# A head's scores as two 128-row products of stacked operands, and the sums of the logs moved amid the gated linear units

## The chip, the cores and the metric

The kernel runs on one core of a Trainium2 chip. It is one program for a transformer of two two-layer blocks (512 tokens, width 1024, float32). The metric is the device time of one execution in microseconds, the median of several runs. Lower is better.

## The reference

The change touches only the mixer of the last layer, `odd_mixer`. It joins two things: an attention with forget gates (8 heads of 64) and a gated convolution over 31 positions.

```
def odd_mixer(x, w_in, forget_b, dw_w, dw_b, cn_g, cn_b, w_out):
    p = x @ w_in                                   # q, k, v: 512 each; 8 forget logits; 2 x 512
    log_f = log_sigmoid(p[..., 1536:1544] + forget_b)
    y_c = forgetting_attention(q, k, v, log_f)
    y_d = conformer_conv(p[..., 1544:], dw_w, dw_b, cn_g, cn_b)
    return concatenate([y_c, y_d]) @ w_out

def forgetting_attention(q, k, v, log_f):
    cum = cumsum(log_f, axis=1)                    # per head
    for each block of 128 queries (q0, q1):
        logits = q[q0:q1] . k[:q1] / sqrt(64)
        logits = logits + cum[q0:q1, None] - cum[None, :q1]
        logits = where(key <= query, logits, -1e30)
        out = softmax(logits) . v[:q1]

def conformer_conv(p_d, dw_w, dw_b, cn_g, cn_b):
    h = p_d[..., :512] * sigmoid(p_d[..., 512:])   # the gated linear unit
    h = causal_dwconv(h, dw_w) + dw_b              # 31 taps per channel
    return silu(layer_norm(h, cn_g, cn_b))
```

## The kernel before, in words

Every float32 product is made from three fp32r products. Each operand is cut into a high part (rounded to fp32r by ScalarE) and a low part (the rest, a subtraction on VectorE, or on GpSimd for the weights named in `ONPOOL`), and `mm3` (L369 to L373) adds high·high, high·low and low·high in PSUM. Weights come by DMA in units of up to 1024 columns and are split one or two units ahead (L170 on ScalarE, L171 on VectorE or GpSimd). The plan of the weights fixes the order in which they are loaded, and `OTHERWISE` names by number the units split on the other engine.

In `odd()` the channels lie on the partitions in four groups of 128, the tokens along the free axis. The order of the instructions is written out by hand, as a sequence of `step(taps, us)`. A step first takes some `us` microseconds of TensorE products out of a list of waiting projections (`fill`), then emits the work that earlier steps left with `done` (evictions, the softmax of a block), then splits a weight unit if fewer than `AHEAD` are ready, then emits `taps` taps of the convolution on VectorE (`tap`, L1376, one fused multiply-add of 128x512 each; channel groups 0 to 2 in turn) and a share of a tap of group 3, which ScalarE multiplies into a tile `tp` (L1381) and GpSimd adds to the sum `cv` (L1382).

The order in the mixer before:

- The gates of channel groups 0 and 1 (their products ran at the end of the layer before), then the products of the gated linear units 2 and 3 (`glu`, 96 products of 512 columns) in steps of 1.8 taps.
- The values and the forget logits (`od_v`, 4 units, 96 products of 264 columns), then on VectorE and ScalarE the log of the sigmoid as a chain of small operations on 128x32 (`log_sigmoid`).
- 32 products of the first pair of heads' queries and keys (`pair(0)`), then `sums()`: two small products that sum the logs over the tokens. They wait for the log chain. VectorE then adds the blocks up and `spread(0)` lays the cumulative sums (high and low part) and ones into the tiles `ab`, which TensorE transposes (`rows(0)`) into four bias rows per head for heads 0 to 3. Heads 4 to 7 follow in `rows(1)` during head 1.
- The heads, one after the other: in the turn of head h TensorE makes the scores of head h+1 block by block (128, 256, 384, 512 keys), attends head h to the values, and transposes the probabilities of head h+1; the projections of later pairs, of the other values and of the output are the filling.

A block of scores is five products into one PSUM bank (L1574 to L1576): three fp32r products over the 64 rows of the head (high and low of query and key: `qh`, `ql`, and the same for keys), one product over the 4 bias rows (L1575), and the causal mask as a bf16 product with the identity over 128 columns. Two heads share a projection: head 2p lies on partitions 0 to 63 of the `pair` tiles, head 2p+1 on 64 to 127. One split of 128x512 on ScalarE (L381 or L378) and one on VectorE (L382 or L379) serve both heads.

In the trace PE is TensorE, DVE VectorE, ACT ScalarE, POOL GpSimd.

Of the kernel before, what the change touches and what calls it, by code (L numbers as in the profile page):

```python
# [9 lines left out]
F32 = mybir.dt.float32  # L10
# [32 lines left out]
for _k, _w in (("g_q", 3), ("g_kv", 2), ("g_sub", 1), ("conv_w", 12), ("pool_s", 4), ("dw_w", 124),  # L43
# [11 lines left out]
OTHERWISE = (11, 12, 15, 20, 23, 24, 25, 73, 79, 80, 81, 82, 83, 84, 85, 86, 88, 90, 91, 100, 102, 103, 224, 226, 231)  # L55
# [9 lines left out]
    "pre": (2.6, 3.4, 2.2, 2.2),  # L65
    "glu": 1.8,
    "v": 2.5,
    "pool0": 0.35,
# [169 lines left out]
def weight_plan(a):  # L238
# [53 lines left out]
    for j in range(4):  # L292
        if j < 2:
            add("od_a", a["od_d"][0, j])
        add("od_g" if j < 2 else "od_x", a["od_d"][1, j])
        if j > 1:
            add("od_x", a["od_d"][0, j])
    for u in range(4):
        add("od_v", a["od_v0"][u])
    for x in "0" + ORDER:  # L300
# [13 lines left out]
def kernel(ctx: ExitStack, tc: tile.TileContext, a: dict, out: bass.AP):  # L314
# [1011 lines left out]
    def odd(xT, open_x, FIRST, names):  # L1326
        with pool("odd") as op_:
# [42 lines left out]
            def tap(j, k, pool=False):  # L1370
                w, x = par("dw_w", CONV * j + k), gl[j][:, k:k + S]
                if not pool:
                    if k == 0:
                        nc.vector.tensor_scalar(cv[j], x, w, par("dw_b", j), op0=OP.mult, op1=OP.add)
                    else:
                        nc.vector.scalar_tensor_tensor(cv[j], x, w, cv[j], op0=OP.mult, op1=OP.add)  # L1376
                elif k == 0:
                    nc.scalar.activation(cv[j], x, AF.Identity, scale=w, bias=par("dw_b", j))
                else:
                    tp = op_.tile([P, S], F32, name="tp", tag="tp", bufs=2)  # L1380
                    nc.scalar.activation(tp, x, AF.Copy, scale=w)  # L1381
                    nc.gpsimd.tensor_add(cv[j], cv[j], tp)  # L1382
# [49 lines left out]

            def pair(p):
                got = []
                while p > 1 and 2 * p - 3 not in SCORED:
                    yield None
                for s in range(2):
                    ps = acc()
                    yield from steps_T(ps, ("od_q", "od_k")[s])
                    hi = ov.tile([P, S], F32R, name="qh", tag=f"qh{s}", bufs=2)  # L1440
                    lo = ov.tile([P, S], F32R, name="ql", tag=f"ql{s}", bufs=2)
                    got += [hi, lo]
                    done(lambda hi=hi, lo=lo, ps=ps, s=s: split(hi, lo, ps, -0.125 if s == 0 else None))
                done(lambda: Q.update({p: got}))
                MADE.add(p)
# [23 lines left out]
            fill = Fill([glu(2), glu(3)])  # L1469
# [4 lines left out]
            while fill.parts:  # L1474
                step(OD["glu"], 1.3)
            fill.parts.extend([pair(0)] + [others() if x == 'v' else pair(int(x)) for x in ORDER])
# [23 lines left out]
            def sums():  # L1500
# [6 lines left out]
                def add():  # L1507
# [7 lines left out]
                    spread(0)  # L1515
# [7 lines left out]
            ab = [op_.tile([P, NT, 4, 32], F32, name=f"ab{i}", tag=("yh", "yl")[i], bufs=4) for i in range(2)]  # L1523
            for i in range(2):
                nc.gpsimd.memset(ab[i], 0.0)
                nc.gpsimd.memset(ab[i][:, :, :, 2 * i:2 * i + 2], 1.0)
            AB = {}

            def spread(g):
                c, h = cum[:, :, 4 * g:4 * g + 4], f32(cumh[:, :, 4 * g:4 * g + 4])  # L1530
                nc.vector.tensor_copy(ab[1][:, :, :, 0], h)
                nc.vector.tensor_sub(ab[1][:, :, :, 1], c, h)
                nc.vector.tensor_scalar(ab[0][:, :, :, 2], h, -1.0, None, op0=OP.mult)
                nc.vector.tensor_sub(ab[0][:, :, :, 3], h, c)

            def rows(g):
                for i in range(2):
                    ps = pst()
                    for t in range(NT):
                        nc.tensor.transpose(ps[:, t * P:(t + 1) * P], ab[i][:, t].rearrange("p h r -> p (h r)"), ident)  # L1540
                    AB[g, i] = op_.tile([P, S], F32R, name="rows", tag=f"rows{i}", bufs=2)
                    done(lambda x=AB[g, i], ps=ps: nc.scalar.activation(x, ps, AF.Copy))
                if g == 0:
                    done(lambda: spread(1))
# [19 lines left out]
            def score(h, qb):  # L1564
                if h > 7:
                    return
                p, i = divmod(h, 2)
                qh, ql, kh, kl = Q[p]
                ms = slice(64 * i, 64 * i + 64)
# [72 lines left out]
            rows(0)  # L1642
            step(1, 1.0)
            step(1, 1.0)
            C, OUT = [], {}
            for h in range(-1, 8):
# [5 lines left out]
                if h == 1:  # L1652
                    rows(1)
# [232 lines left out]
```

## Time and profile before

| | us |
|---|---|
| median of 3 runs (lowest, highest) | 2301.66 (2300.28, 2306.31) |
| the profiled execution | 2304.18 |
| its span | 2302.4 |
| TensorE busy over the span | 2250.3 (98%) |
| VectorE, ScalarE, GpSimd busy | 1770.4 (77%), 997.1 (43%), 471.3 (20%) |
| granted clock over the span | 0.989 |

The profile gives the busy time of each engine over a stretch, the waits with what ended them, and a timeline of single instructions. The granted clock is the share of full speed (2.4 GHz) that TensorE was given: 0.50 means 1.2 GHz. TensorE's products are pipelined, so the duration of one is longer than the distance to the next: what a product takes is read from the distance of the starts. The touched part of the mixer lies from 1701.04 us (the first product of the gated linear units) to 1891.94 us (the end of the last head's turn).

### The profile page before, as it was taken

What the parts mean: (1) busy time and instruction counts of PE and PEld (TensorE: products, weight loads), DVE (VectorE), ACT (ScalarE), POOL (GpSimd) and SP (SyncE); (2) the same over time, 40 slices, a digit from 0 to 9 for tenths busy, and PEclk for the clock granted to TensorE, in tenths of its full rate; (3) what the DMA queues carried; (4) which work ended last, traced back from release to release, by engine and by line L of the source; (5) the groups of instructions that cost most, each with busy time, mean ns of one, the idle gap of its engine ahead of it and who ended that gap; (6) DMA issues with size and microseconds to landing.
All of it is one profiled execution on the core that took longest, in us unless ns stands there. A gap on an engine that the chain in (4) does not pass through costs nothing. (4 is left out here: it accounts for less than half of the span.)

```text
span 2302.4 us, 35345 instructions
## 1 busy us (share of the span) xinstructions
PE 2250.3 (98%) x14148; PEld 1988.6 (86%) x14148; DVE 1770.4 (77%) x2718; ACT 997.1 (43%) x1665; POOL 471.3 (20%) x280
## 2 busy tenths in 40 slices
PE   8999999999999999999999999999998999999997
PEld 8878999998888789999988899999886768999996
DVE  5667888886656688888765588888767766988886
ACT  4654444333555554443333244434334654444341
POOL 2200111113321111111210011111246531111112
PEclk9999999999999999999999999999998989999999
DMA  5112233332222033333233233332232112233321
GB/s 180 55 45 92 92 106 105 111 92 90 92 66 73 28 110 101 102 110 109 86 106 100 64 129 110 110 101 92 83 96 74 37 37 101 92 110 110 101 92 65
DMA packets 59365, 210.51 MB, mean 91 GB/s; under 512 B 6624, under 2 KB 6880, under 8 KB 59200
## 3 DMA queue, kind: packets, MB, share of 16 engines
q1 hardware_dynamic: 56304, 198.97, 27.5%
q0 software_dynamic: 2320, 8.23, 1.1%
q8 instruction: 111, 1.82, 0.3%
q10 hardware_dynamic: 576, 1.05, 0.1%
q14 instruction: 54, 0.44, 0.1%
HBM read 206.12 MB, written 2.10 MB: 90 GB/s over the span
## 5 line engine op out<-in xcount | busy, mean ns | idle before, releaser
L170 ACT ACTIVATE whi<-wraw 128x1024 fp32r<-128x1024 f32 (+3 forms) x528 | 521.0, 989 | 831.0 <-PE acc L372 301.3
L171 POOL TENSOR_TENSOR wlo<-wraw,whi 128x1024 fp32r<-128x1024 f32 (+2 forms) x141 | 355.8, 2526 | 1281.4 <-ACT whi L170 1030.2
L171 DVE TENSOR_TENSOR wlo<-wraw,whi 128x1024 fp32r<-128x1024 f32 (+3 forms) x387 | 429.3, 1110 | 136.8 <-ACT whi L170 136.1
L371 PE MATMUL acc<-xh,whi 128*128 128x256 f32 (+1 forms) x1712 | 527.3, 308 | 0.0
L372 PE MATMUL acc<-xl,whi 128*128 128x256 f32 (+1 forms) x1712 | 524.2, 306 | 3.1 <-DVE xl L481 3.1
L373 PE MATMUL acc<-xh,wlo 128*128 128x256 f32 (+1 forms) x1712 | 522.8, 305 | 3.1 <-DVE wlo L171 3.1
L372 PEld LDWEIGHTS acc<-xl,whi 128*128 128x128 f32 x1712 | 322.9, 189 | 28.5 <-DVE xl L481 4.3
L371 PEld LDWEIGHTS acc<-xh,whi 128*128 128x128 f32 x1712 | 322.9, 189 | 24.8 <-issue 0.9
L373 PE MATMUL acc<-xs,wlo 128*128 128x256 f32 x1216 | 342.6, 282 | 0.0
L372 PE MATMUL acc<-xql,whi 128*128 128x256 f32 x1216 | 341.4, 281 | 0.0
L371 PE MATMUL acc<-xs,whi 128*128 128x256 f32 x1216 | 340.0, 280 | 0.4 <-ACT sums L768 0.4
L373 PEld LDWEIGHTS acc<-xh,wlo 128*128 128x128 f32 x1712 | 322.9, 189 | 20.0 <-DVE wlo L171 4.1
L371 PEld LDWEIGHTS acc<-xs,whi 128*128 128x128 f32 x1216 | 229.9, 189 | 4.4 <-ACT sums L768 0.8
L372 PEld LDWEIGHTS acc<-xql,whi 128*128 128x128 f32 x1216 | 228.5, 188 | 5.7
L373 PEld LDWEIGHTS acc<-xs,wlo 128*128 128x128 f32 x1216 | 228.4, 188 | 0.0
L371 PE MATMUL tr<-whi,hh 128*128 128x512 f32 (+1 forms) x296 | 118.1, 399 | 0.0
L372 PE MATMUL tr<-wlo,hh 128*128 128x512 f32 (+1 forms) x296 | 116.9, 395 | 0.0
L373 PE MATMUL tr<-whi,hl 128*128 128x512 f32 (+1 forms) x296 | 115.8, 391 | 0.0
L373 PE MATMUL ps<-whi,hl 128*128 128x512 f32 x288 | 113.7, 395 | 0.0
L371 PE MATMUL ps<-whi,hh 128*128 128x512 f32 x288 | 113.2, 393 | 0.0
L372 PE MATMUL ps<-wlo,hh 128*128 128x512 f32 x288 | 113.2, 393 | 0.0
L431 DVE SCALAR_TENSOR_TENSOR res<-res,acc 128x512 f32<-128x512 f32 x87 | 58.9, 683 | 55.2 <-PE acc L373 54.9
(353 smaller groups left out, 4195.6 us busy)
## 6 DMA issues: line engine op xcount, KB each, us to landing
wraw<-in_gu_dram SPq DMA_DIRECT2D x176, 512.0 KB, 3.7
wraw<-in_dn_dram SPq DMA_DIRECT2D x88, 512.0 KB, 3.4
wraw<-in_ev_in_dram SPq DMA_DIRECT2D x16, 512.0 KB, 3.5
wraw<-in_mla_o_dram SPq DMA_DIRECT2D x8, 512.0 KB, 3.5
wraw<-in_df_q_dram SPq DMA_DIRECT2D x8, 512.0 KB, 3.4
wraw<-in_df_k_dram SPq DMA_DIRECT2D x8, 512.0 KB, 3.5
wraw<-in_df_v_dram SPq DMA_DIRECT2D x8, 512.0 KB, 3.4
wraw<-in_df_o_dram SPq DMA_DIRECT2D x8, 512.0 KB, 3.4
```

The costliest lines, as they stand in the source:

```text
L170: self.nc.scalar.activation(hi, raw[:, o:o + n], AF.Copy)
L171: eng.tensor_sub(lo, raw[:, o:o + n], hi.bitcast(F32))
L371: nc.tensor.matmul(ps, ah, bh, start=first, stop=False)
L372: nc.tensor.matmul(ps, ah, bl, start=False, stop=False)
L373: nc.tensor.matmul(ps, al, bh, start=False, stop=last)
L431: nc.vector.scalar_tensor_tensor(y, y, ALPHA if first else 1.0, ps, op0=OP.mult, op1=OP.add, accum_out=SUMS[t][:, c:c + 1] if sums else None)
```

## The change

The three 64-row products and the 4-row product of a score block become two products over all 128 rows. For each head the kernel keeps four 128x512 operands in `STACK` (two sets, by the parity of the pair): `qa` and `kb` hold the high parts of query and key on the head's own 64 partitions, and on the other 64 the bias rows (`qa` those of all heads; `kb` those of this head alone, the others multiplied by zero with the selector `own_rows`); `qq` holds high and low of the query, `kk` low and high of the key. So `qa·kb` is high·high plus the bias, and `qq·kk` is the two cross products. The mask product stays.

`place()` takes the part of the split: for a pair ScalarE now runs 8 instructions of 64x512 out of PSUM and VectorE 4, and `bias()` adds 2 on ScalarE; `rows()` runs once, for all 8 heads. The tile `tp` has one buffer where it had two.

The order at the head of the mixer is another: the values and the logs come right after the gates, then the gated linear units 2 and 3 in steps that hold `choose()` (the selector), `sums()` after the sixth step and `rows()` after the ninth, and then `pair(0)`.

```
-    "pre": (2.6, 3.4, 2.2, 2.2),
+    "pre": 1.3,
     "glu": 1.8,
     "v": 2.5,
+    "sums": 6,
+    "rows": 9,
...
-                    tp = op_.tile([P, S], F32, name="tp", tag="tp", bufs=2)
+                    tp = op_.tile([P, S], F32, name="tp", tag="tp", bufs=1)
...
+            def place(p, s, ps):
+                for m in range(2):
+                    qa, qq, kb, kk = STACK[p % 2][m]
+                    own, other = HALF[m], HALF[1 - m]
+                    if s == 0:
+                        nc.scalar.activation(qq[own], ps[own], AF.Copy, scale=-0.125)
+                        nc.vector.scalar_tensor_tensor(qq[other], ps[own], -0.125, f32(qq[own]), op0=OP.mult, op1=OP.subtract)
+                    else:
+                        nc.scalar.activation(kb[own], ps[own], AF.Copy)
+                        nc.vector.tensor_sub(kk[own], ps[own], f32(kb[own]))
+                for m in range(2):
+                    qa, qq, kb, kk = STACK[p % 2][m]
+                    own, other = HALF[m], HALF[1 - m]
+                    if s == 0:
+                        nc.scalar.activation(qa[own], ps[own], AF.Copy, scale=-0.125)
+                    else:
+                        nc.scalar.activation(kk[other], ps[own], AF.Copy)
+
+            def bias(p):
+                for m in range(2):
+                    h, other = 2 * p + m, HALF[1 - m]
+                    nc.scalar.activation(STACK[p % 2][m][2][other], f32(ROWS["k"][other]), AF.Copy, scale=own_rows[other, h:h + 1])
...
+            def choose():
+                nc.vector.tensor_reduce(own_rows, rows_of[0], axis=mybir.AxisListType.X, op=OP.add)
+                nc.vector.tensor_reduce(lf[:, 4, 0], rows_of[1], axis=mybir.AxisListType.X, op=OP.add)
+                nc.vector.tensor_add(own_rows, own_rows, lf[:, 4, 0])
...
-                mm3(ps[:, :n], qh[ms, qs], ql[ms, qs], kh[ms, :n], kl[ms, :n], True, False)
-                r = slice(32 * (h % 4), 32 * (h % 4) + 4)
-                nc.tensor.matmul(ps[:, :n], AB[h // 4, 0][r, qs], AB[h // 4, 1][r, :n], start=False, stop=False)
+                nc.tensor.matmul(ps[:, :n], qa[:, qs], kb[:, :n], start=True, stop=False)
+                nc.tensor.matmul(ps[:, :n], qq[:, qs], kk[:, :n], start=False, stop=False)
                 nc.tensor.matmul(ps[:, qs], idb, mkb, start=False, stop=True)
...
-            step(1, OD["pre"][0])
-            step(1, OD["pre"][1])
-            sums()
-            step(1, OD["pre"][2])
-            step(1, OD["pre"][3])
+            fill.parts.extend([glu(2), glu(3)])
+            n = 0
+            while fill.parts:
+                step(OD["glu"], 1.3)
+                n += 1
+                if n == 1:
+                    choose()
+                if n == OD["sums"]:
+                    sums()
+                if n == OD["rows"]:
+                    rows()
+            fill.parts.extend([pair(0)] + [others() if x == 'v' else pair(int(x)) for x in ORDER])
+            while 0 not in MADE:
+                step(OD["pre"], 1.3)
             have(0)
...
-            rows(0)
-            step(1, 1.0)
-            step(1, 1.0)
...
-                if h == 1:
-                    rows(1)
```

On TensorE, a block of head 0's scores against 512 keys in the program's order, before (`ps` is the bank of the scores, `acc` that of a projection, `mkb` and `idb` the mask and the identity):

```order
L373 MATMUL acc<-xh,wlo 128x512
L371 MATMUL ps<-qh 128x512
L372 MATMUL ps<-ql,qh 128x512
L373 MATMUL ps<-qh,ql 128x512
L1575 MATMUL ps<-rows 128x512
L1576 LDWEIGHTS idb
L1576 MATMUL ps<-mkb,idb 128x128
L371 MATMUL acc<-xh,whi 128x512
```

The same block of the changed kernel:

```order
L375 MATMUL acc<-xh,wlo 128x512
L1616 MATMUL ps<-kb_17072,qa_17070 128x512
L1617 MATMUL ps<-kk_17073,qq_17071 128x512
L1618 LDWEIGHTS idb
L1618 MATMUL ps<-mkb,idb 128x128
L373 MATMUL acc<-xh,whi 128x512
```

Two products of 512 columns leave the block; the products of the projections round it stay.

On VectorE, from the end of the log chain (`lf`) to the tiles `ab` that are transposed, before:

```order
L1498 SCALAR_TENSOR_TENSOR lf<-lf 128x32
L1376 SCALAR_TENSOR_TENSOR cv_17064<-gl_17060,sm,cv_17064 128x512
L1376 SCALAR_TENSOR_TENSOR cv_17062<-gl_17058,sm,cv_17062 128x512
L382 SCALAR_TENSOR_TENSOR ql<-acc,qh 128x512
L1376 SCALAR_TENSOR_TENSOR cv_17063<-gl_17059,sm,cv_17063 128x512
L1509 COPY lf<-ps 128x32
L1510 COPY lf<-ps 128x32
...
L1534 TENSOR_TENSOR ab_17231<-cumh,lf 128x16
```

And of the changed kernel (at the "..." stand nine more taps, in the same turn of `cv_17062` and `cv_17063`; L1378 is the tap, L1561 to L1563 `choose()`):

```order
L1527 SCALAR_TENSOR_TENSOR lf<-lf 128x32
L1378 SCALAR_TENSOR_TENSOR cv_17063<-gl_17059,sm,cv_17063 128x512
L1561 TENSOR_REDUCE own_rows<-ident 128x8
L1562 TENSOR_REDUCE lf<-ident 128x8
L1563 TENSOR_TENSOR own_rows<-own_rows,lf 128x8
L1378 SCALAR_TENSOR_TENSOR cv_17062<-gl_17058,sm,cv_17062 128x512
...
L1378 SCALAR_TENSOR_TENSOR cv_17062<-gl_17058,sm,cv_17062 128x512
L1538 COPY lf<-ps 128x32
L1539 COPY lf<-ps 128x32
...
L1570 TENSOR_TENSOR ab_17097<-cumh,lf 128x8x8
```

Where three taps and the low part of a query stood before the copies of the sums, there now stand twelve taps and the selector.

On ScalarE, the keys of a pair, before:

```order
L1065 ACTIVATE pth_18180<-tr 128x128
L170 ACTIVATE whi<-wraw 128x1024
L1065 ACTIVATE pth_18180<-tr 128x2x128
L378 ACTIVATE qh<-acc 128x512
L1381 ACTIVATE tp<-gl_17061,sm 128x512
L1065 ACTIVATE pth_18180<-tr 128x2x128
```

And of the changed kernel (`pth` is the transposed probabilities, evicted by the same engine):

```order
L1067 ACTIVATE pth_18167<-tr 128x128
L1451 ACTIVATE kb_17072<-acc 64x512
L1451 ACTIVATE kb_17076<-acc 64x512
L1459 ACTIVATE kk_17073<-acc 64x512
L1459 ACTIVATE kk_17077<-acc 64x512
L1465 ACTIVATE kb_17072<-rows,own_rows 64x512
L1465 ACTIVATE kb_17076<-rows,own_rows 64x512
L1067 ACTIVATE pth_18165<-tr 128x2x128
```

Six instructions stand where one stood, and the next eviction of probabilities stands behind them.

## Rows read from the trace of the kernel before

**Rows 1.** Page, busy time of the engines over the whole span.

```profile
PE 2250.3 (98%) x14148; PEld 1988.6 (86%) x14148; DVE 1770.4 (77%) x2718; ACT 997.1 (43%) x1665; POOL 471.3 (20%) x280
```

**Rows 2.** Windows: stretch, length, busy PE, PEld, DVE, ACT, POOL; clock, DMA, GB/s.

```profile
1701.04:1765.56 64.52, 54.58 (x267) 46.24 (x265) 52.32 (x88) 19.11 (x30) 30.44 (x17) 0.89 0.23 71
1765.56:1780.63 15.07, 15.07 (x74) 10.79 (x73) 10.77 (x23) 9.48 (x24) 10.74 (x6) 1.00 0.26 67
1780.63:1813.33 32.70, 32.25 (x204) 26.43 (x204) 25.53 (x47) 24.21 (x59) 21.63 (x14) 1.00 0.12 35
1813.33:1845.98 32.65, 32.65 (x146) 23.19 (x145) 24.78 (x45) 21.33 (x52) 17.81 (x11) 0.90 0.11 33
1845.98:1870.17 24.19, 22.49 (x100) 15.92 (x99) 15.99 (x40) 17.63 (x44) 11.67 (x7) 0.86 0.15 44
1870.17:1891.94 21.77, 19.07 (x79) 13.60 (x79) 12.82 (x26) 11.45 (x25) 4.77 (x2) 0.84 0.16 49
```

**Rows 3.** Waits of PE, 1690 to 1950 us: us in all, times, longest.

```profile
PE ps L1504 <- issue: 6.6, 1, 6.6
PE acc L372 <- POOL wlo L171: 3.4, 1, 3.4
PE acc L373 <- DVE yl L379: 1.8, 1, 1.8
```

**Rows 4.** Windows behind the two longest waits, columns as in rows 2.

```profile
1736.00:1742.00 6.00, 6.00 (x26) 5.81 (x27) 0.66 (x3) 2.12 (x4) 3.73 (x2) 0.50 0.50 175
1755.30:1759.00 3.70, 3.70 (x11) 3.12 (x12) 3.23 (x10) 0.35 (x2) 0.00 (x0) 0.50 0.02 4
```

**Rows 5.** Timeline round the log chain: start, length, engine, line, operation, tiles.

```profile
1746.68 5.21 POOL L171 TENSOR_TENSOR wlo<-wraw,whi 128x1024 fp32r<-128x1024 f32 x2 [2.58 <-ACT whi L170]
...
1747.27 2.37 DVE L1493 TENSOR_TENSOR lf<-lf 128x32 f32<-128x32 f32 x1
...
1755.12 1.41 DVE L1376 SCALAR_TENSOR_TENSOR cv<-gl,sm,cv 128x512 f32<-128x512 f32 x2
1756.44 0.68 DVE L382 SCALAR_TENSOR_TENSOR ql<-acc,qh 128x512 fp32r<-128x512 f32 x1
...
1757.70 0.18 DVE L1509 COPY lf<-ps 128x32 f32<-128x32 f32 x1
...
1759.22 0.18 DVE L1534 TENSOR_TENSOR ab<-cumh,lf 128x16 f32<-128x16 f32 x1
```

**Rows 6.** Timeline, PE, head 1's block against 512 keys.

```profile
1786.55 0.28 PE L373 MATMUL acc<-whi,xl 128*128 128x256 f32 x1
...
1787.10 0.39 PE L372 MATMUL ps<-ql,qh 64*128 64x512 f32 x1
1787.33 0.39 PE L373 MATMUL ps<-qh,ql 64*128 64x512 f32 x1
1787.65 0.49 PE L1575 MATMUL ps<-rows 4*128 4x512 f32 x1
1788.08 0.23 PE L1576 MATMUL ps<-mkb,idb 128*128 128x128 bf16 x1
1788.11 0.36 PE L371 MATMUL acc<-whi,xh 128*128 128x256 f32 x1
```

**Rows 7.** Timeline, PE, head 4's block against 128 keys.

```profile
1829.94 0.40 PE L373 MATMUL acc<-xh,wlo 128*128 128x512 f32 x1
...
1830.43 0.27 PE L372 MATMUL ps<-ql,qh 64*128 64x128 f32 x1
1830.54 0.27 PE L373 MATMUL ps<-qh,ql 64*128 64x128 f32 x1
...
1831.03 0.48 PE L371 MATMUL acc<-xh,whi 128*128 128x512 f32 x1
```

**Rows 8.** Timeline, ScalarE, two copies of 128x512 in a row.

```profile
1763.12 1.09 ACT L1542 ACTIVATE rows<-tr 128x512 fp32r<-128x512 f32 x2
```

**Rows 9.** Groups, GpSimd, 1765.56 to 1884.4 us: busy, mean ns, idle before.

```profile
L1382 POOL TENSOR_TENSOR cv<-cv,tp 128x512 f32<-128x512 f32 x27 | 42.3, 1566 | 36.1 <-ACT tp L1381 35.7
```

More of the change, by code (lines that the diff above doesn't have):

```diff
@@ L54 @@
 ONPOOL = ("od_x", "od_v", "od_q", "od_k", "od_o", "uq_n", "ukv", "df_o", "mla_o", "down")
-OTHERWISE = (11, 12, 15, 20, 23, 24, 25, 73, 79, 80, 81, 82, 83, 84, 85, 86, 88, 90, 91, 100, 102, 103, 224, 226, 231)
+OTHERWISE = (11, 12, 15, 20, 23, 24, 25, 73, 79, 80, 81, 82, 83, 84, 85, 86, 88, 90, 91, 100, 102, 103, 224, 226, 227)
 NORM_ACT = (1, 3, 6, 7, 12, 13, 16, 24, 25, 26, 30)
@@ L291, in weight_plan @@
     ffn("2", 0)
[L292 to L297, printed above, removed]
+    for j in range(2):
+        add("od_a", a["od_d"][0, j])
+        add("od_g", a["od_d"][1, j])
     for u in range(4):
         add("od_v", a["od_v0"][u])
+    for j in range(2, 4):
+        add("od_x", a["od_d"][1, j])
+        add("od_x", a["od_d"][0, j])
     for x in "0" + ORDER:
@@ L1431, in odd @@
             Q, MADE, SCORED = {}, set(), set()
+            STACK = [[[ov.tile([P, S], F32R, name=f"{n}{b}{m}") for n in ("qa", "qq", "kb", "kk")]
+                      for m in range(2)] for b in range(2)]
+            ROWS = {}
+            def place(p, s, ps):
[19 more added lines that the diff above has]
+                    nc.scalar.activation(STACK[p % 2][m][2][other], f32(ROWS["k"][other]), AF.Copy, scale=own_rows[other, h:h + 1])
             def pair(p):
-                got = []
                 while p > 1 and 2 * p - 3 not in SCORED:
@@ L1439, in pair @@
                     yield from steps_T(ps, ("od_q", "od_k")[s])
[L1440 to L1444, printed above, removed]
+                    done(lambda ps=ps, s=s: place(p, s, ps))
+                if p:
+                    done(lambda: bias(p))
+                done(lambda: Q.update({p: STACK[p % 2]}))
                 MADE.add(p)
@@ L1467, in have @@
                     step(1)
-            fill = Fill([glu(2), glu(3)])
+            fill = Fill([])
             region = ExitStack()
@@ L1473, in odd @@
                 gate(j, *FIRST[2 * j:2 * j + 2])
-            while fill.parts:
-                step(OD["glu"], 1.3)
-            fill.parts.extend([pair(0)] + [others() if x == 'v' else pair(int(x)) for x in ORDER])
             vh = op_.tile([P, NT, S], F32R, name="vh")
@@ L1514, in add @@
                     nc.scalar.activation(cumh, cum, AF.Copy)
-                    spread(0)
+                    spread()
                 done(add)
             cumh = op_.tile([P, NT, 8], F32R, name="cumh")
-            ab = [op_.tile([P, NT, 4, 32], F32, name=f"ab{i}", tag=("yh", "yl")[i], bufs=4) for i in range(2)]
+            own_rows = op_.tile([P, 8], F32, name="own_rows")
+            rows_of = [ident[:, 64 * i:64 * i + 32].rearrange("p (h r) -> p h r", r=4) for i in range(2)]
+            ab = [op_.tile([P, NT, 2, 16, 4], F32, name=f"ab{i}", tag=("yh", "yl")[i], bufs=4) for i in range(2)]
@@ L1536, in rows, with spread @@
-            def rows(g):
+                nc.gpsimd.memset(ab[i][:, :, :, 0:8, 2 * i:2 * i + 2], 1.0)
+            def choose():
+                nc.vector.tensor_reduce(own_rows, rows_of[0], axis=mybir.AxisListType.X, op=OP.add)
+                nc.vector.tensor_reduce(lf[:, 4, 0], rows_of[1], axis=mybir.AxisListType.X, op=OP.add)
+                nc.vector.tensor_add(own_rows, own_rows, lf[:, 4, 0])
+            def spread():
+                c, h = [x[:, :, None, :].to_broadcast([P, NT, 2, 8]) for x in (cum, f32(cumh))]
+                nc.vector.tensor_copy(ab[1][:, :, :, 0:8, 0], h)
+                nc.vector.tensor_sub(ab[1][:, :, :, 0:8, 1], c, h)
+                nc.vector.tensor_scalar(ab[0][:, :, :, 0:8, 2], h, -1.0, None, op0=OP.mult)
+                nc.vector.tensor_sub(ab[0][:, :, :, 0:8, 3], h, c)
@@ L1537, in rows @@
+            def rows():
+                got = []
                 for i in range(2):
-                    ps = pst()
+                    got.append(pst())
                     for t in range(NT):
-                        nc.tensor.transpose(ps[:, t * P:(t + 1) * P], ab[i][:, t].rearrange("p h r -> p (h r)"), ident)
-                    AB[g, i] = op_.tile([P, S], F32R, name="rows", tag=f"rows{i}", bufs=2)
-                    done(lambda x=AB[g, i], ps=ps: nc.scalar.activation(x, ps, AF.Copy))
@@ L1543, in rows, with put @@
-                if g == 0:
-                    done(lambda: spread(1))
+                        nc.tensor.transpose(got[i][:, t * P:(t + 1) * P], ab[i][:, t].rearrange("p d h r -> p (d h r)"), ident)
+                def put():
+                    ROWS["k"] = op_.tile([P, S], F32R, name="rows", tag="yh", bufs=4)
+                    nc.scalar.activation(ROWS["k"], got[1], AF.Copy)
+                    for b in range(2):
+                        for m in range(2):
+                            other = HALF[1 - m]
+                            nc.scalar.activation(STACK[b][m][0][other], got[0][other], AF.Copy)
+                        if b == 0:
+                            bias(0)
@@ L1546, in value @@
+                done(put)
             def value(t, ps):
@@ L1566, in score @@
                     return
-                p, i = divmod(h, 2)
-                qh, ql, kh, kl = Q[p]
-                ms = slice(64 * i, 64 * i + 64)
+                qa, qq, kb, kk = Q[h // 2][h % 2]
                 n = (qb + 1) * P
```

8 lines of the change are left out of this document (removed).

## The prediction, on record before the run

> **What bounds the kernel now.** The page's busy times come first: TensorE works 98% of the span [rows 1], so time can leave only where TensorE does less, waits less or runs at a higher clock. The windows over the last mixer say which of the three each stage offers [rows 2]. In the first, up to the first score, TensorE is idle for 64.52 − 54.58 = 9.9 us. In the two that follow it is busy throughout at a clock of 1.00: there only fewer products help. In the last three the clock is 0.90, 0.86 and 0.84. The list of waits [rows 3] names the idle time of the first window: 6.6 us before the sums of the logs (L1504) and 3.4 us for a weight that GpSimd splits; the 1.8 us for `yl` lies in the last one. Behind the two long waits the granted clock was 0.50, which is 1.2 GHz, for 6.0 and 3.7 us [rows 4]: half of that, 4.9 us, is lost against 2.4 GHz. The timeline round the logs [rows 5] shows that the chain itself is stretched: one operation on 128x32 took 2.37 us where its like take 0.18, while GpSimd split weights.
>
> **Part 1: the score blocks.** A block costs what lies between the starts of the filling products on both sides, less one of them. Against 512 keys: 1788.11 − 1786.55 = 1.56, less 0.12 for a product of 256 columns (half of the 0.23 between the two 512-wide starts at 1787.10 and 1787.33), 1.44 us [rows 6]. Against 128 keys: 1831.03 − 1829.94 = 1.09, less 0.23, 0.86 us [rows 7]. The blocks of 256 and 384 taken on the line between, 1.05 and 1.25, a head costs 4.6 us. The products themselves are less than that: where the height changes from 64 to 4 to 128 rows, starts stand 0.32 and 0.43 apart instead of 0.23. Afterwards a block has two full-height products and the mask (0.04, the distance from its start to the next): 0.50, 0.42, 0.34 and 0.26, in sum 1.5 us a head if nothing is lost at the switches, 2.3 if each block still loses 0.2. The saving is 2.3 to 3.1 us a head; I take 2.8, since same-height neighbours in these rows lose nothing. Over eight heads: 22.4 (18.4 to 24.8).
>
> A rule could make it less. In head 1's block the 4-row product reads other partitions (32 to 35) than the head's 64, and the mask still starts 0.43 us behind it [rows 6]. The Trainium skill (TensorE: Matmul & The Clock Gate, "Why this matters for your kernels") says that products of few rows in distinct row groups run at the same time; were that so here, four of the eight heads would already have their bias for nothing and the change would save there about 0.23 + 0.17 + 0.12 + 0.06 = 0.6 us a head less. The row shows the full price, so the sum goes by 2.8.
>
> **Part 2: the other engines, pair by pair.** For a pair ScalarE ran 2 instructions of 512 columns, now 10. Two such copies in a row took 1.09 us, 0.545 each [rows 8], so a pair costs 8 × 0.545 = 4.4 us more; the price of 64 partitions is not below that of 128 in any row here, and I take it as equal. VectorE's splits go from 2 to 4 at 0.68 [rows 5]: 1.4 more. `rows(1)` goes (2 copies, 1.1 us). Three pairs are made behind the first score, so ScalarE gets 3 × 4.4 − 1.1 = 12.1 us of work there.
>
> Now each window of [rows 2] as the largest of three: TensorE's length less 2.8 a head; VectorE's and ScalarE's busy time with the additions.
> - Head 0: 15.07 − 2.8 = 12.3; VectorE 10.8, ScalarE 9.5. Gain 2.8.
> - Heads 1 and 2: TensorE 32.70 − 5.6 = 27.1; VectorE 25.5 + 1.4 = 26.9; ScalarE 24.2 + 4.4 − 1.1 = 27.5. I take 27.5: gain 5.2.
> - Heads 3 and 4: TensorE 27.1 at the same clock; VectorE 26.2, ScalarE 25.7. With three engines that near each other something waits; I take 27.5, gain 5.1.
> - Heads 5 and 6: TensorE 24.19 − 5.6 = 18.6; ScalarE 17.6 + 4.4 = 22.0, of which some two of its ten instructions fall into the stretch before: 21.0, gain 3.2.
> - Head 7 and the last turn: 21.77 − 2.8 for the scores, − 1.8 for `yl` and its like (three taps that stood before it are gone in the order, 3 × 0.66 = 2.0), less some of the low clock (0.16 × 21.77 = 3.5 lost, a fifth of it back, 0.7): 16.5, gain 5.3.
>
> Together 21.6 behind the first score: nearly all of what TensorE saves.
>
> **Part 3: the head of the mixer.** Instructions move here, and the waits move with them. Before: from the last `od_v` product to the sums 32 products × 0.23 = 7.4 us and the wait of 6.6: the log chain takes 14.0 us. After, 36 products stand there, 8.3 us, so the chain still ends last and 5.7 us are waited. From 1747.27 to the end of GpSimd's two weight splits at 1746.68 + 5.21 = 1751.89 VectorE got through two small operations of that chain, worth 0.4 [rows 5], so about 4.2 of the 14.0 is blocking; if GpSimd has nothing to split just then, the wait is 1.5. Behind the chain VectorE has 12 taps and `choose()` ahead of the copies of the sums; before it had 3 taps and one split. A tap is (1756.44 − 1755.12) / 2 = 0.66 us, so 7.9; three small operations at 0.18, 0.5; copies to `ab` 1759.22 + 0.18 − 1757.70 = 1.7 [rows 5]. That is 10.1 us, and TensorE has 18 products (4.1 us) until it needs `ab` for the transposes. So a wait of about 6 us appears at `rows()` that was not there. The stage added up:
> - `od_v`, 96 products of 264 columns at 0.12: 11.5. GpSimd's 3.4 us wait [rows 3] I count as gone, because the four narrow units now stand in its queue without a 1024-wide one among them; it may stay, 0 to 3.4.
> - chain to the sums 14.0 (9.8 unblocked), sums to `ab` 10.1, eight transposes at 0.11: 0.9.
> - the other 42 + 48 + 6 = 96 products of 512: 22.1.
> - two waits of 6 us with half clock behind them, as in [rows 4] but half of it hidden in what waits anyway: 2.4 (0 to 4.9).
> - the first score waits for four copies of the last key (4 × 0.545 = 2.2) behind 6 products (1.4): 0.8.
>
> In sum 61.8 against 64.5: gain 2.7, from −1 (GpSimd's wait stays) to +8 (unblocked, no half clock). What is worth most in this part, to have the sums done under other work, I expect to be eaten by the taps in VectorE's queue.
>
> **The sum.** 2.7 + 2.8 + 5.2 + 5.1 + 3.2 + 5.3 = 24.3. From the profiled execution, 2304.2 − 24.3 = 2279.9. That execution was 2.5 us above the median of the runs, so against the median 2277.4 us, 1.05% below 2301.66. With the bounds of the parts (18 to 25 for the scores, −1 to +8 for the head) the forecast's own range is 2268 to 2288.
>
> **Rivals.**
> - *The clock comes back.* The low clock in the last three windows costs 0.10 × 32.65 + 0.14 × 24.19 + 3.5 = 10.2 us. Its stretches stand behind no long wait; what fills them are score blocks back to back. If products of 64 and 4 rows are what lets the clock fall, full-height ones bring it back, and if ScalarE keeps up: 22.4 + 10.2 + 1.8 + 2.7 = 37.1, 2264.6 us. Against: ScalarE's 22.0 in heads 5 and 6, and shorter blocks wait more, not less. The Trainium skill's rule (same page and section) names idle gaps of TensorE as what drops its clock; the two stretches behind waits agree with it [rows 4], the last three windows are not explained by it, and by it more waiting there would lower the clock further.
> - *TensorE's saving is lost to the queues.* If ScalarE's six instructions in a row hold up the probabilities of the head in turn (6 × 0.545 = 3.3 us, at two places per pair, three pairs, 20 us), nearly all of the 21.6 is given back and the head of the mixer gains nothing: 24.3 − 20 = 4, 2297.7. For it: order puts them directly before evictions that TensorE waits for. Against: a turn has about 12 us of other products.
> - *Slower: one buffer for `tp`.* ScalarE may write the next `tp` only when GpSimd has added the last, and stands still meanwhile with softmax and splits behind it. At the worst each of the 27 sums of 1.566 us [rows 9] is waited out: 42.3 us. ScalarE has 84.1 us of work in the last five windows [rows 2], 96.2 after, and the windows last 126.4; it sets the pace above the old one from (126.4 − 96.2) / 27 = 1.1 us of wait per sum on. In full: 96.2 + 42.3 = 138.5, 12.1 longer, less 2.7 for the head: +9.4, 2311 us. Against: 27 in 119 us are 4.4 us apart in the mean.
>
> **How the numbers follow.** The forecast has 0.66, the clock 0.14, the queues 0.13, the single buffer 0.07. What a measurement of this kernel can tell from no change is 0.3%, 6.9 us. Faster is the forecast and the clock with a little of the queues' case: 0.81. Same is most of the queues' case: 0.12. Slower is the buffer: 0.07. The range takes in the clock's 2264.6 and the queues' 2297.7 less its far side: 2262 to 2297.
>
> **What the new profile would show.** Right: distances of 0.23 between the two score products and blocks of 0.5 us or a little more against 512 keys; a wait before L1504's successor of about 6 us and a second one of about 6 before the transposes; busy shares of VectorE and ScalarE over 0.9 in heads 1 to 4. Wrong: a switch cost of 0.4 or more per block (gain under 18); no wait at the transposes (VectorE ran its taps earlier than its order lets me think); a clock of 1.00 from head 3 on; or waits named after `tp` on ScalarE of more than 1 us each.

## The result, and the profile after

The changed kernel took 2327.51 us (median of 4 runs, 2325.11 to 2329.46), the kernel before 2303.98 in the runs beside it (2300.28 to 2310.22): a ratio of 1.0099, 95% interval [1.0073, 1.0125]. It is slower by 23.5 us. The forecast was 24 us faster, and the range, up to 2297, did not hold the result.

The page's busy times, beside [rows 1]:

```profile
PE 2232.8 (96%) x14076; PEld 1980.0 (85%) x14076; DVE 1779.9 (77%) x2725; ACT 1019.8 (44%) x1700; POOL 466.3 (20%) x280
```

TensorE is busy 17.5 us less, and the span is 20.9 us longer: it waits. The windows between the same places as in [rows 2], and the rest of the program (columns as there):

```profile
1702.12:1769.05 66.93, 52.93 (x260) 44.33 (x259) 62.59 (x95) 24.84 (x36) 28.02 (x12) 0.87 0.24 71
1769.05:1791.45 22.40, 15.22 (x64) 11.80 (x65) 11.79 (x20) 15.12 (x31) 11.58 (x7) 0.77 0.23 70
1791.45:1825.65 34.20, 27.98 (x184) 25.11 (x182) 23.91 (x48) 25.96 (x58) 19.69 (x13) 0.90 0.11 32
1825.65:1863.41 37.76, 27.31 (x129) 20.23 (x128) 23.42 (x48) 26.34 (x59) 16.82 (x10) 0.86 0.09 29
1863.41:1897.94 34.53, 21.40 (x88) 16.69 (x86) 18.67 (x44) 24.88 (x58) 13.28 (x8) 0.75 0.09 30
1897.94:1913.15 15.21, 14.88 (x73) 11.26 (x72) 6.69 (x20) 11.16 (x25) 4.78 (x2) 0.89 0.14 41
1913.15:2323.00 409.85, 394.76 (x2609) 358.06 (x2607) 337.66 (x444) 152.97 (x202) 75.96 (x38) 0.99 0.30 95
```

The same rest in the kernel before:

```profile
1891.94:2302.00 410.06, 395.64 (x2609) 359.67 (x2607) 336.98 (x444) 153.24 (x202) 76.20 (x38) 0.98 0.30 94
```

Nearly all of the difference, 20.1 us of it, is in the touched part: 211.0 us against 190.9 [rows 2]. By window it is +2.4, +7.3, +1.5, +5.1, +10.3 and −6.6. TensorE's busy time there is 159.7 against 176.1, its idle time 51.3 against 14.8. Only the last window, in which no pair is made, comes out near its forecast: 15.2 us, and 16.5 was the number. The five windows behind the first score last 144.1 us together, where 104.8 were worked out; the first lasts 66.9 where 61.8 were.

The granted clock was 0.50 (1.2 GHz) for the 10.3 us from the first score on, with a wait of 5.4 us ahead of it and one of 5.5 in it:

```profile
1769.05:1779.30 10.25, 4.72 (x14) 3.76 (x15) 6.65 (x9) 5.19 (x9) 5.37 (x3) 0.50 0.16 51
```

It was 0.50 again from 1871.6 to 1878.3 and from 1885.2 to 1895.3; waits of 5.4 and 3.9 us ended at 1872.2 and 1885.1.

What TensorE waited for (us in all, times, longest), where [rows 3] named three waits:

```profile
PE tr L1054 <- DVE ptl L1069: 9.1, 5, 2.5
PE ps L1616 <- ACT kb L1465: 9.0, 2, 5.1
PE ps L1616 <- ACT e L1631: 8.1, 3, 5.4
PE ps L1533 <- issue: 6.3, 1, 6.3
PE ps L1617 <- ACT kk L1459: 5.5, 1, 5.5
PE ps L1616 <- ACT kb L1451: 5.4, 1, 5.4
PE ps L373 <- ACT e L1631: 4.5, 2, 4.1
PE tr L1577 <- DVE ab L1570: 2.3, 1, 2.3
```

Four of the eight name operands or exponentials that ScalarE is late with at a score, 28 us in sum; the longest row is VectorE's eviction of transposed probabilities. ScalarE's timeline shows why it is late. The queries of the second pair (start, length, engine, line; in brackets the idle time before it and what ended it):

```profile
1784.34 0.58 ACT L1448 ACTIVATE qq<-acc 64x512 fp32r<-64x512 f32 x1
1785.68 0.59 ACT L1448 ACTIVATE qq<-acc 64x512 fp32r<-64x512 f32 x1 [0.75 <-DVE qq L1449]
1787.03 1.20 ACT L1457 ACTIVATE qa<-acc 64x512 fp32r<-64x512 f32 x2 [0.76 <-DVE qq L1449]
```

And the keys of the first pair, with the first score waiting behind them:

```profile
1768.41 0.59 ACT L1451 ACTIVATE kb<-acc 64x512 fp32r<-64x512 f32 x1
1773.06 0.59 ACT L1451 ACTIVATE kb<-acc 64x512 fp32r<-64x512 f32 x1 [4.06 <-DVE kk L1452]
1774.41 1.21 ACT L1459 ACTIVATE kk<-acc 64x512 fp32r<-64x512 f32 x2 [0.76 <-DVE kk L1452]
```

The two engines take turns: ScalarE's copy for the second head stands until VectorE has subtracted for the first, though it needs nothing of it; then again. Where VectorE is free a turn costs 0.75 us; where taps stand ahead of the subtraction, ScalarE stands behind them too, and everything queued on ScalarE with it. `place()` writes the four operations in that order (ScalarE, VectorE, ScalarE, VectorE), all of them read one PSUM bank, and the trace has ScalarE released by VectorE at exactly these copies. That the shared bank is what links them is inferred: the two heads write different tiles, and nothing else joins the two operations. The split of the kernel before had one instruction on each engine, so its pairs never met this.

Ahead of the first keys' subtraction (1772.34) VectorE had five taps, the second row here. The first row is eleven taps ahead of the copies of the sums, while GpSimd was idle (1726.2 to 1738.98):

```profile
1729.49 7.37 DVE L1378 SCALAR_TENSOR_TENSOR cv<-gl,sm,cv 128x512 f32<-128x512 f32 x11
1764.81 7.50 DVE L1378 SCALAR_TENSOR_TENSOR cv<-gl,sm,cv 128x512 f32<-128x512 f32 x5
```

That is 0.67 us a tap with GpSimd idle, and 1.50 beside two additions and a weight split on GpSimd.

The score block itself did what was forecast. Head 1 against 512 keys, as in [rows 6]:

```profile
1794.93 0.28 PE L375 MATMUL acc<-whi,xl 128*128 128x256 f32 x1
1795.05 0.40 PE L1616 MATMUL ps<-kb,qa 128*128 128x512 f32 x1
1795.29 0.40 PE L1617 MATMUL ps<-kk,qq 128*128 128x512 f32 x1
1795.53 0.23 PE L1618 MATMUL ps<-mkb,idb 128*128 128x128 bf16 x1
1795.56 0.36 PE L373 MATMUL acc<-whi,xh 128*128 128x256 f32 x1
```

1795.56 − 1794.93 − 0.12 = 0.51 us, where it was 1.44, with 0.24 between the starts and nothing lost at switches.

ScalarE's own waits from 1762 to 1904 us, from just before the first score into the last head's turn:

```profile
ACT tp L1383 <- POOL cv L1384: 8.2, 12, 1.4
ACT e L1631 <- DVE sums L1630: 7.3, 5, 2.2
ACT kb L1451 <- DVE kk L1452: 6.4, 4, 4.1
ACT qq L1448 <- DVE qq L1449: 5.2, 4, 2.5
ACT e L1627 <- DVE sums L1623: 4.6, 17, 0.9
ACT kk L1459 <- DVE kk L1452: 3.0, 4, 0.8
ACT qa L1457 <- DVE qq L1449: 3.0, 4, 0.8
```

Turns take 17.6 us (four rows), the single `tp` 8.2.

### The profile page after: what moved, and what is told of

Same layout as the page of the kernel before. It is cut to its first block, busy times and chain, and to the rows that moved or that the text cites. A ratio compares the mean times of both kernels' runs of the same rounds, so it can differ in the third digit from the quotient of the medians.

```text
span 2323.3 us, 35207 instructions
## 1 busy us (share of the span) xinstructions
PE 2232.8 (96%) x14076; PEld 1980.0 (85%) x14076; DVE 1779.9 (77%) x2725; ACT 1019.8 (44%) x1700; POOL 466.3 (20%) x280
## 5 line engine op out<-in xcount | busy, mean ns | idle before, releaser
L172 ACT ACTIVATE whi<-wraw 128x1024 fp32r<-128x1024 f32 (+2 forms) x528 | 520.2, 987 | 836.1 <-DMA wraw<-in_gu_dram 273.1
L196 DVE TENSOR_TENSOR wraw<-wraw 128x512 f32<-128x512 f32 x76 | 121.1, 1593 | 0.0
```

The lines of the kernel that those rows point to most:

```text
L172: self.nc.scalar.activation(hi, raw[:, o:o + n], AF.Copy)
L196: nc.vector.tensor_sub(a21, a11, a21)
```

## The experiments

Theories: **turns** (place()'s alternation), **amount** (ScalarE's added instructions), **one tp**, **move** (the new order at the head) and **no room** (TensorE's saving is lost anyway, since a head's turn is then as long as its softmax's way through the other engines). Times are medians; the kernel before lay at 2302.9 to 2304.7 beside these runs.

**The halves of the change.** Stacked scores in the old order; the move with the old scores.

```
# e3: the weights' plan, glu, od_v, pair(0), sums() and rows() in the old order
# e4: the kernel before, with od_v first, sums() and rows(0) amid glu(2), glu(3)
```

> The changed kernel's stacked scores and place() as they are, with the order at the head of the mixer of the kernel before (gated linear units first, then the values, the sums amid the first pair, rows() behind it). Theory 'turns': the taking of turns stays, so it stays slower than before, 2312 to 2330. Theory 'amount': the same, it cannot be told from 'turns' here. Theory 'move': the loss was in the new order, so this one is near the forecast for the scores alone, 2280 to 2290.

> The kernel before with only the order at the head of the mixer changed as in the change (values first, sums in the sixth and the first bias rows in the ninth step of the gated linear units); scores by five products, the split by one instruction on each engine. Theories 'turns' and 'amount': the move alone costs nothing or little, 2298 to 2309. Theory 'move': it carries the loss, 2318 to 2330.

Measured 2320.2 (ratio 1.0082 [1.0060, 1.0104]) and 2312.3 (1.0048 [1.0029, 1.0067]). Both halves lose: 17.1 and 9.2, in sum 26, near the whole 23.5. For the move, between the ranges of both theories, a row of TensorE's waits says where:

```profile
PE ps L372 <- DVE ql L379: 11.6, 1, 11.6
```

From the start of the touched part to the first score e4 takes 3.7 us less than the kernel before (60.8 against 64.5). Then TensorE stands between the first and the second product of that score for the split of the first keys, behind taps on VectorE, of which five took 11.07 us while GpSimd worked beside them:

```profile
1755.66 4.96 POOL L171 TENSOR_TENSOR wlo<-wraw,whi 128x1024 fp32r<-128x1024 f32 x1 [11.70 <-ACT whi L170]
1760.58 3.38 POOL L1382 TENSOR_TENSOR cv<-cv,tp 128x512 f32<-128x512 f32 x2
1763.92 5.54 POOL L171 TENSOR_TENSOR wlo<-wraw,whi 128x1024 fp32r<-128x1024 f32 x2
```

VectorE in the same stretch:

```profile
1758.93 11.07 DVE L1376 SCALAR_TENSOR_TENSOR cv<-gl,sm,cv 128x512 f32<-128x512 f32 x5
```

**The taps put off.**

```
-    "taps": (0.4, 0.9, 0.7, 0.7, 0.9, 0.4, 0.2, 0.2, 1.6),
+    "taps": (0.4, 0.9, 0.7, 0.7, 0.9, 0.7, 0.6, 0.6, 1.6),
-    "pre": 1.3,
+    "pre": 0.0,
```

> The kernel with the move alone (2312.3), and the taps during the first pair's products (1.3 a step) are put off into the heads 5 to 7 (0.4, 0.2, 0.2 a step become 0.7, 0.6, 0.6). Theory 'taps in front of the first split' (TensorE's 11.6 us before the first score is VectorE's queue): that wait goes to under 4 us, and the time falls by 5 to 10 us, 2302 to 2307. Theory 'the weights or the clock': no change, 2309 to 2316.

Measured 2308.9 (1.0015 [1.0002, 1.0028]). That row of TensorE's waits became

```profile
PE ps L372 <- DVE ql L379: 2.5, 2, 2.1
```

so the cause of that wait is shown. By the medians 3.4 us came home, below the expectation. Between the two products e14 takes 0.7 us where e4 took 11.9. From the second product of the first score to the end of the last head's turn, e4 and then e14 (columns as in [rows 2]):

```profile
1770.66:1901.52 130.86, 127.10 (x601) 93.05 (x602) 79.53 (x166) 84.41 (x199) 63.90 (x37) 0.89 0.12 37
1764.41:1897.58 133.17, 127.62 (x601) 93.11 (x602) 94.60 (x178) 87.76 (x202) 71.77 (x40) 0.88 0.14 44
```

So 11.2 us went between the two products, and 2.3 came back behind them, where the twelve put-off taps now stand. The touched part of these two executions differs by 8.9 us (203.5 and 194.7), more than the medians do; e14's began 4.9 us later in its execution, ahead of anything that the edit changes. The taps are worth some 3 to 9 us, then. In both kernels this stretch is longer than the 126.2 us of the kernel before, at a clock of 0.89 and 0.88 instead of 0.92; that part of the move's cost has no cause shown.

**Turns.** In the changed kernel, in the stack with the old order, and in the kernel before.

```
# e1, e8: place(), first loop over m
-    nc.scalar.activation(qq[own], ...); nc.vector.scalar_tensor_tensor(qq[other], ...)
# ScalarE's four copies of both heads first, then VectorE's two subtractions
# e6: the kernel before
-    split(hi, lo, ps, scale)
+    for m in range(2): split(hi[HALF[m]], lo[HALF[m]], ps[HALF[m]], scale)
# e7: the same halves, ScalarE's two first, then VectorE's two
```

> The changed kernel with one edit: in place() ScalarE's four copies are written ahead of VectorE's two subtractions, so the same instructions run in another order. Theory 'turns' (ScalarE's second copy waits for VectorE's first subtraction, because both read the same bank, and so ScalarE stands in line behind VectorE's taps): the idle time of ScalarE before L1451, L1448 and their like goes from about 13 us to near 0, the waits of TensorE for kb and kk (20 us) mostly go, and the time falls by 12 to 30 us, to 2297 to 2315. Theory 'amount' (ScalarE simply has ten instructions a pair instead of two): the order inside place() changes nothing, 2322 to 2331. Theory 'move' (the new order at the head of the mixer costs it): likewise no change.

> Stacked scores with the old order at the head of the mixer (2320.2 as measured), and with ScalarE's four copies of place() ahead of VectorE's two subtractions. Theory 'turns': 8 to 12 us come back, 2308 to 2313, and ScalarE's waits for kk and qq are gone. Theory 'turns alone explain the loss of the stack': it falls to the forecast for the scores, 2280 to 2285. Theory 'amount': 2317 to 2322.

> The kernel before with one edit: a pair's split is done by halves of 64 partitions in turns, ScalarE, VectorE, ScalarE, VectorE, as place() does; nothing is stacked, the scores stay, and ScalarE has only 2 instructions more per pair for each half. Theory 'turns': ScalarE waits before its second half for VectorE's first, 8 times, 0.75 us where VectorE is free and several us where taps stand ahead; the kernel becomes slower by 5 to 15 us, 2308 to 2320. Theory 'amount': 2 x 0.5 us a pair more on ScalarE, at most 3 us in all, 2303 to 2307.

> The control to the run with the halves in turns: the kernel before, a pair's split by halves of 64 partitions, but ScalarE's two first and VectorE's two behind. The same instructions and counts, without the taking of turns. Theory 'turns': most of the 11 us goes away, 2302 to 2308. Theory 'amount' (one more instruction of each engine a split): it stays at 2310 to 2318.

e1: 2319.0, 8.5 less than the changed kernel, and short of the expected 12 to 30. The copies now stand next to each other:

```profile
1827.19 1.19 ACT L1448 ACTIVATE qq<-acc 64x512 fp32r<-64x512 f32 x2
1828.39 1.20 ACT L1455 ACTIVATE qa<-acc 64x512 fp32r<-64x512 f32 x2
```

e8: 2310.4, 9.8 less than e3. e6: 2314.5 (1.0055 [1.0033, 1.0077]), 11 slower than before, by the turns of plain halves and the second instruction on each engine together. e7, which has those instructions without the turns, lies between the two expectations: 2309.9, but its ten runs spread from 2305.4 to 2319.4, five of them under 2309 and three over 2317, so it settles little; e1 and e8, which change the order alone, carry the proof. Turns cost 8 to 10 us there; they are not the whole.

**One tp.**

```
-    tp = op_.tile([P, S], F32, name="tp", tag="tp", bufs=2)
+    tp = op_.tile([P, S], F32, name="tp", tag="tp", bufs=1)
```

> The kernel before with one buffer for tp instead of two, nothing else. In the changed kernel ScalarE stands 8.2 us before its writes of tp, waiting for GpSimd's additions; in the kernel before 0. Theory 'one tp' (the single buffer carries a part of the loss by itself): slower by 4 to 10 us, 2307 to 2313, with waits of ScalarE for GpSimd of 5 to 10 us. Theory 'turns and amount': ScalarE has room for it here, no change within 3 us, 2300 to 2306.

Measured 2308.4 (1.0021 [1.0008, 1.0033]): 5.5 us, by the interval 1.8 to 7.6, with ScalarE waiting 7.6 us for GpSimd before `tp` where it waited for nothing there before. The profiled executions show 2.9 of the 5.5 from the first score to the end of the last head (129.3 against 126.4).

**TensorE's saving alone, and the copies.**

```
# e16: the kernel before, score()
-    mm3(qh[ms, qs], ql[ms, qs], kh[ms, :n], kl[ms, :n]); matmul of the 4 bias rows
+    matmul(qh[:, qs], kh[:, :n]); matmul(ql[:, qs], kl[:, :n])   # all 128 rows
# e17: e8 without the copies to qa[own], kk[other], kb[other]
```

> The kernel before, in which a score block is two products over all 128 rows of the tiles that are there already, and the mask (the bias and one cross product are left out, and two heads are mixed, so the scores are not the reference's). No operand is stacked, ScalarE, VectorE and GpSimd have exactly their old work: TensorE's saving by itself. The forecast's step (TensorE saves 2.8 us a head and the other engines leave room for nearly all of it, 21.6 us behind the first score): 2279 to 2285. Theory 'no room' (the turn of a head is already nearly as long as the softmax's way through VectorE and ScalarE, so the freed time turns into waits): 2290 to 2300.

> Stacked scores in the old order with ScalarE's copies first (2310.4), and the duplicates and the bias copies of a pair left out (zeros stand there, so the scores are not the reference's): ScalarE has 4 instructions of 64x512 a pair instead of 10. Theory 'amount': the 6 instructions a pair, 18 behind the first score at 0.59 and 0.72 us, are 11.5 us of ScalarE's time and most of that comes back, 2297 to 2303. Theory 'no room' alone: little comes back, 2305 to 2311.

e16: 2294.0 (0.9959 [0.9945, 0.9972]): with nothing added to any engine, the saving is worth 9.4 us, not 21.6. From the first score to the end of the last head, the window of the kernel before:

```profile
1765.56:1891.94 126.38, 121.52 (x597) 89.92 (x597) 89.89 (x177) 84.09 (x199) 66.62 (x37) 0.92 0.15 42
```

The same window of e16:

```profile
1770.20:1885.28 115.08, 96.10 (x535) 76.31 (x534) 87.99 (x177) 82.72 (x200) 67.79 (x38) 0.96 0.15 46
```

The stretch is 11.3 us shorter in these two executions; the medians differ by 9.4. TensorE is busy 25.4 us less and idle 14.1 us more (19.0 against 4.9). VectorE and ScalarE have 88 and 83 us in 115, so neither is full; but TensorE now waits for them where it had other products before (e16's waits):

```profile
PE ps L1573 <- ACT e L1588: 7.8, 6, 1.8
...
PE tr L1052 <- DVE ptl L1067: 5.4, 4, 2.4
```

e17: 2301.2, 9.2 less than e8: the copies of the duplicates and the bias cost that much.

**Which queue.** The duplicates on GpSimd; from there without the taps of GpSimd, or without VectorE's.

```
# e9: e8 with
+    nc.gpsimd.tensor_copy(qa[own], f32(qq[own])); nc.gpsimd.tensor_copy(kk[other], f32(kb[own]))
# e11: e9, tap(pool=True) with k > 0 issues nothing     # e12: e9, no taps on VectorE from the first head on
```

> As the run before it in this list, and the two duplicates of each half (qa from qq, kk from kb) are copied by GpSimd instead of ScalarE: ScalarE's instructions for a pair fall from 10 to 6, GpSimd's rise by 4 of about 0.6 us. Theory 'amount' (ScalarE's work in the turn of a head is what lasts): 12 instructions of 0.59 us off its path, 5 to 10 us faster than without, 2300 to 2306. Theory 'chain' (the softmax of a head waits from engine to engine and TensorE has too little filling left): little change, within 4 us. It could also cost, since VectorE's taps run longer while GpSimd works: up to 5 us.

> As the run with the duplicates on GpSimd (2306.6), and the taps of channel group 3 that ScalarE multiplies and GpSimd adds are left out (part of the convolution isn't computed). ScalarE loses 28 instructions of 0.72 us (20 us in eight heads) and all its waits for GpSimd (9.5 us). Theory 'amount' (ScalarE's queue is what a head's turn lasts): the time falls by 12 to 25 us, to 2282 to 2295. Theory 'chain' (the softmax goes from engine to engine and back, whatever else is queued): it falls by less than 6 us, 2300 to 2307.

> As the run with the duplicates on GpSimd (2306.6), and VectorE's taps are left out from the first head on (part of the convolution isn't computed): about 48 instructions of 0.66 us or more. Theory 'taps in front' (the evictions of the probabilities and the minima of the softmax stand behind taps in VectorE's queue, TensorE's 13.1 us before the transposes being that): falls by 15 to 30 us, to 2277 to 2292. Theory 'amount' (ScalarE is it): falls by less than 8 us, 2298 to 2307.

e9: 2306.6, 3.8 less than e8. e11: 2289.7. e12: 2290.5. Both fall by 16 to 17, where each theory had expected that only one would. e12 takes work from VectorE alone. e11 doesn't do the same for ScalarE: the additions go from GpSimd too, and VectorE's taps from the first score on (busy, mean ns) ran faster without them, in e9 and then in e11:

```profile
L1378 DVE SCALAR_TENSOR_TENSOR cv<-gl,sm,cv 128x512 f32<-128x512 f32 x45 | 48.7, 1085 | 0.2
L1378 DVE SCALAR_TENSOR_TENSOR cv<-gl,sm,cv 128x512 f32<-128x512 f32 x44 | 37.7, 859 | 0.2
```

So e11's 17 us are ScalarE's, GpSimd's and VectorE's together; for ScalarE alone e17 stands, with its 9.2. With that, ScalarE's and VectorE's queues both lie on the way of a head, and work taken from either shortens it.

**All mends.** e15: new order, grouped copies, duplicates on GpSimd, taps put off. e18: e9 with a second tile for `tp` up to head 5. e19: e18 with the bias copies on GpSimd.

```
# e18
+    tp = ab[1] viewed as [P, S] at every second tap (the bias rows are transposed by then)
# e19, bias()
-    nc.scalar.activation(kb[other], f32(ROWS["k"][other]), AF.Copy, scale=own_rows[other, h:h + 1])
+    nc.gpsimd.tensor_scalar(kb[other], f32(ROWS["k"][other]), own_rows[other, h:h + 1], None, op0=OP.mult)
```

> The changed kernel (2327.5) with the three mends together: ScalarE's copies ahead of VectorE's subtractions, duplicates on GpSimd, and the taps of the first pair's products put off to heads 5 to 7. If the three causes add up: 2327.5 - 8.5 - 4 - 8 = 2307, 2301 to 2311. If the put-off taps only come back as waits in the heads: 2311 to 2318. Below the kernel before (under 2298) only if the heads have room that none of the runs so far shows.

> The run with old order, grouped copies and duplicates on GpSimd (2306.6), and up to head 5 ScalarE writes tp by turns into two tiles (the second is the tile ab of the bias rows, free by then). If the single buffer costs here what it cost alone (5 us): 2300 to 2304, and ScalarE's 9.5 us of waits for GpSimd fall under 4. If the single buffer only cost where nothing else held ScalarE: 2305 to 2308.

> The run before it in this list, and the two bias copies of a pair (0.72 us each on ScalarE, 6 behind the first score) are done by GpSimd. If ScalarE's queue is still what lasts: 2 to 4 us faster than without. If GpSimd, which then has 4 duplicates, 2 bias copies and the taps of group 3, becomes the one that is waited for: slower by 2 to 6 us.

e15: 2311.5 (1.0037 [1.0022, 1.0051]), 0.5 over the range of causes that add up. That the put-off taps come back as waits in the heads isn't shown: TensorE is idle 27.7 us from the first score on, and 33.1 in e1. e18: 2300.9 (0.9989 [0.9979, 0.9998]), 5.7 less than e9, and ScalarE's waits for `tp` are gone: the best of the stacked kernels that leave nothing out, 2.5 us below the kernel before, by an interval that just clears 1. e19: 2313.8, worse by 13, more than either side expected: GpSimd took 1.65 us for a copy that ScalarE did in 0.72, and TensorE waits for it. GpSimd's group of these copies (busy, mean ns, idle before):

```profile
L1476 POOL TENSOR_SCALAR kb<-rows,own_rows 64x512 fp32r<-64x512 f32 x8 | 13.2, 1656 | 0.7
```

The row of TensorE's waits:

```profile
PE ps L1630 <- POOL kb L1476: 8.3, 3, 4.6
```

## Why the prediction was wrong

The pieces, each measured in runs of their own, add up to the result: TensorE's saving −9.4 (e16), turns +9.8 (e3 to e8), copies +9.2 (e8 to e17), one `tp` +5.5 (e5), the move +9.2 (e4): +24.3 against the measured +23.5. Single medians move by some 2 us, and the pieces were taken in different kernels: within the stacked ones the move costs 7.3 (e3 to the changed kernel) or 8.6 (e8 to e1) and the turns 8.5 (e1). So that the sum fits so well is partly luck; the signs and rough sizes are not.

- **Part 1 (the score blocks) was right.** 0.51 us for the wide block where 0.50 was worked out, and 25.4 us less of TensorE's time in e16 (its mean clock there rose from 0.92 to 0.96) where 22.4 were taken.
- **Part 2 failed, and with it the forecast.** The step "each window as the largest of three" took an engine's busy time as the least that a window can last. A head's turn is a path instead: score, minimum on VectorE, exponential on ScalarE, reciprocal, scaling, transposes, evictions on both, values. TensorE's products covered it, and with fewer of them in a turn they cover less. With no other cost 14.1 of 25.4 us turned into waits. The gain of 21.6 should have been 9 to 11, less what the added instructions cost. The sign that the forecast named, VectorE and ScalarE busy over 0.9 in heads 1 to 4, stayed away: their shares there are 0.62 to 0.76.
- **Part 2 also priced place() as a count.** A pair takes ScalarE 5.0 us more where 4.4 were worked out (eight copies at 0.59, the two of the bias at 0.72, less two at 0.59), and from the first score on it is busy 103.5 us, not 96.2; 15.1 of that lie in head 0's window, to which the forecast gave 9.5. But the forecast had these instructions hidden, and they were not: e17 gives 9.2 us for 18 of them behind the first score and those ahead of it. The alternation was not seen at all: the code of the change has ScalarE and VectorE in turns on one bank, and the prediction counted instructions without asking what each waits for. The Trainium skill (PSUM — Partial Sum Buffer, "PSUM bank collisions raise a hardware error") says that accesses of two engines to one bank have to be kept apart, reads too, but that different 32-partition quadrants do not collide; by it the wait between the two halves guards more than the chip needs. The runs show only that the wait is there and what it costs; taking the wait alone away wasn't tried.
- **Part 3 (the head) erred in the place of the wait.** The sums waited 6.3 us where 5.7 were worked out, the transposes 2.3 where 6 were. But the first score waited 5.4, and 5.5 more at its second product, where 0.8 stood in the sum: taps stand ahead of the first pair's splits too, five of them between the queries' and the keys', and the prediction followed VectorE's queue only up to `ab`. Those five took 1.50 us each, not 0.66, while GpSimd worked. The Trainium skill (SBUF — State Buffer, "Who interferes with whom") has a VectorE instruction with two SBUF inputs contend with GpSimd's reads; e4's five taps of 11.07 us beside GpSimd's rows agree, and so do the 0.67 and 1.50 us of the changed kernel.
- **The rivals.** "TensorE's saving is lost to the queues" came nearest, as the mechanism that ScalarE's row of copies holds up the head in turn, but it was priced as giving back the gain and no more. "One buffer for tp" was real and cost 5.5, a wait of about 0.3 us per sum, under the point of 1.1 from which it was to decide. "The clock comes back" went the other way: 0.77 and 0.75 in two windows, and TensorE's 159.7 busy us hold about 6 more than the removed work would leave. The Trainium skill's rule on idle gaps that stood beside this rival in the prediction (TensorE: Matmul & The Clock Gate, "Why this matters for your kernels") agrees with the three stretches at 0.50 that go with long waits. In e16, where no wait behind the first score was over 2.4 us, the clock rose from 0.92 to 0.96, although TensorE was idle longer in all: there the rival's sign was right.

## What to carry to other kernels

When an engine that is busy 98% loses work, ask what its products were covering: take the work away in a run that changes nothing else, before paying for it on other engines. Where an eviction is cut into parts, write one engine's reads of a PSUM bank together; parts in turns cost a round trip each (0.75 us here), and a whole queue when the other engine is behind (4.06). A buffer dropped to make room and taps put ahead of a split are part of the price.

## What the runs showed of the hardware

- A ScalarE copy of 64 partitions by 512 took 0.59 us, as one of 128 partitions did (0.60); one out of SBUF with a scale per partition 0.72. GpSimd took 0.69 to 0.75 for a copy of 64x512 (e9) and 1.65 with a multiplication (e19).
- Products of 128 rows beside each other started 0.24 us apart at 512 columns, and no gap showed to the bf16 mask product; in the kernel before starts stood 0.32 and 0.43 us apart, 0.1 to 0.2 more, where 64-row and 4-row products met others.
